# Earlier weight loads and splits for the first gate/up group, and later squares, in a two-layer encoder trunk

## The chip, the cores and the metric

The kernel runs on one core of a Trainium2 chip. The metric is device microseconds (us) of one execution, taken as the median of the runs; less is better.

## The reference

Each of two layers works on x, 256 positions by 2048 channels, in float32:

```
for l in range(DEPTH):
    h = rmsnorm(x, norm1_g[l])
    proj = jnp.einsum('bsd,de->bse', h, w_in[l])
    ...
    a = dilated_attention(q, k, v)
    g = chunked_spatial_gating(uv, gmlp_ln_g[l], w_spatial[l], b_spatial[l])
    mix = jnp.concatenate([rmsnorm(a, ...), rmsnorm(g, ...)], axis=-1)
    x = x + jnp.einsum('bse,ed->bsd', mix, w_out[l])
    h = rmsnorm(x, norm2_g[l])
    ff = jax.nn.silu(jnp.einsum('bsd,df->bsf', h, w_gate[l])) * jnp.einsum('bsd,df->bsf', h, w_up[l])
    x = x + jnp.einsum('bsf,fd->bsd', ff, w_down[l])
return rmsnorm(x, final_g)
```

The feed-forward width is 5632. What matters here is the passage in each layer from the second half of `w_out` (which adds the gMLP half `g` to x) to the first columns of `w_gate` and `w_up`, which need the normalised x.

## The kernel before, in words

**Products.** Every float32 operand is split into a high part (a copy rounded to the type that TensorE takes, made by ScalarE, line 861 for weights) and a low part (the difference, made by VectorE, line 862). A product is three matmuls: high by high, high by low, low by high. Positions lie in two tiles of 128, so four PSUM banks `v`, `z`, `x`, `w` hold two position tiles by two blocks of 512 columns.

**Groups and slots.** The work is a list of groups. In layer 0, groups 5 and 6 are `w_out` for the attention half, groups 7 and 8 (`og`) for the gMLP half, and groups 9, 10, 11 and so on (`ff`) are gate/up blocks of 512 columns each. A group is a list of slots, and slots are the unit of time of the schedule: each slot emits its matmuls, then a side task or two. An ordinary slot `N` is one pair of 128-row blocks for one position tile, so a pair takes two slots (24 matmuls together). In an `ff` group four of the eight pairs are done in a fast form: seven products M1 to M7 (12 matmuls each) of sums of weight blocks (`q11`, `q12`, `q21`, `q22`) with sums of x blocks. The first group of a layer takes the order N N N M1 N M5 M2 M6 M3 M7 M4; later ones take N M1 N M5 M2 N M6 M3 M7 M4 N.

**Loads and splits by slot number.** A weight load (1 MB each, issued by the SP queue) and a weight split have a due slot. Events are sorted by due slot less a lead, 5 slots for a load and 3 for a split (2 for a fast group after the first). At each slot the events that have come up are emitted, if the pool of 17 buffers of 1 MB has room. A load waits on its buffer's last readers. Each engine and queue works in the order of emission.

**What splits do besides.** After M1's split VectorE adds `q12` into `q11` (line 837). After M5's split VectorE adds `q22` into `q11`, and a DMA from GpSimd's queue adds `q22` into `q12` (line 841). After M2's split another such DMA adds `q11` into `q21`: M4's split can only start when it has landed. The sums `q11` of the second kind serve M6.

**The norm.** The x blocks (four of 512 channels) are finished by group 7 (blocks 0, 1) and group 8 (blocks 2, 3). For each block a side task `Norm.block` transposes on TensorE (line 265). Blocks 0 and 1 serve the ordinary pairs. Blocks 2 and 3 serve the fast pairs: ScalarE copies the transposes to a buffer `hr` (lines 328, 329), VectorE forms four sums (line 252), ScalarE splits off the high half of `h` (line 255) and VectorE the low half (line 257). M1 reads block 2 in its first six matmuls and block 3 in the last six. Afterwards `Norm.square` sums squares (line 310, ScalarE); after the last block VectorE and GpSimd make `rstd` (lines 314, 271, 272), which the first `silu` (line 623) needs.

**Banks.** Five PSUM buffers serve `v`, `z`, `x`, `w` and one of the products M1, M5, M6, M7 at a time. M1's and M5's results are copied out by ScalarE (line 917), so M5 can start after M1's copy and M6 after M5's copy. M7 starts after VectorE has added M2's bank (line 937).

The order of emission in one slot `s` is:

```
split_by(s)
while next_event(s, False):
    pass
gr.run(i)
...
run_side()
```

Of the kernel before, what the change touches and what calls it, by code (L numbers as in the profile page):

```python
# [27 lines left out]
KD = D // P  # L28
# [3 lines left out]
KR = 4  # L32
# [31 lines left out]
LA_LOAD = 5  # L64
LA_SPLIT = 3
# [38 lines left out]
def encoder_kernel(ctx: ExitStack, tc: tile.TileContext, x, xf, w, ws, lng, cols, fg, cs, msk, out):  # L104
# [18 lines left out]

    early = cpool.tile([P, 1], F32, name="early")
    nc.scalar.activation(out=early, in_=ones, func=AF.Copy)
    warm = sdp.tile([P, P], F32, tag="sd", name="warm")
    for _ in range(WARM):
# [29 lines left out]
    def gcol(l, which, k):  # L157
        return colt[:, l * GC + {"n1": 0, "a": KD, "g": KD + 8, "n2": KD + 16}[which] + k:][:, 0:1]
# [51 lines left out]
    def put_split(kt, k, src, g):  # L210

        hi = kt.t[:, k, 0, :]
        nc.scalar.activation(out=hi, in_=src, func=AF.Copy, scale=g)
        nc.vector.scalar_tensor_tensor(
            out=kt.t[:, k, 1, :], in0=src, scalar=g, in1=hi.bitcast(F32), op0=ALU.mult, op1=ALU.subtract
        )
        kt.ready[k] = True

    def put_splits(kt, k, ps, gs):

        src = [ps[:, j].rearrange("p t q -> p (t q)") for j in range(2)]
        for j in range(2):
            nc.scalar.activation(out=kt.t[:, k + j, 0, :], in_=src[j], func=AF.Copy, scale=gs[j])
        for j in range(2):
            nc.vector.scalar_tensor_tensor(
                out=kt.t[:, k + j, 1, :], in0=src[j], scalar=gs[j], in1=kt.t[:, k + j, 0, :].bitcast(F32),
                op0=ALU.mult, op1=ALU.subtract,
            )
            kt.ready[k + j] = True
# [14 lines left out]
    def sums(raw, n, dst):  # L244

        r = raw.view("p (j f q) -> p j f q", j=2, f=8)[:, :n]
        f = lambda i: r[:, :, i, :]
        for to, a, op, b in (
            (3, f(7), ALU.subtract, f(2)), (4, f(3), ALU.subtract, f(0)),
            (5, f(0), ALU.subtract, f(7)), (6, f(1), ALU.add, f(4)),  # L250
        ):
            nc.vector.tensor_tensor(out=f(to), in0=a, in1=b, op=op)
        src = r[:, :, 0:7, :].rearrange("p j f q -> p j (f q)")
        hi, lo = (dst.rearrange("p (j h z) -> p j h z", h=2, z=7 * P)[:, :, i] for i in range(2))
        nc.scalar.activation(out=hi, in_=src, func=AF.Copy)  # L255
        yield 1
        nc.vector.tensor_tensor(out=lo, in0=src, in1=hi.bitcast(F32), op=ALU.subtract)  # L257
        raw.free()

    def transposes(src, k, name):  # L260

        ps = sdp.tile([P, 2, NT, P], F32, tag="sd", name=name)
        for j in range(2):
            for t in range(NT):
                nc.tensor.transpose(ps[:, j, t, :], src[:, t, (k + j) * P:(k + j + 1) * P], ident)  # L265
        return ps
# [8 lines left out]
    class Norm:  # L275
# [41 lines left out]
        def block(self, b):  # L317

            fast = [p for p in (2 * b, 2 * b + 1) if p >= self.slow]
            raw = Big(f"hr_{self.which}_{self.l}_{b}") if fast else None  # L320
            ps = [transposes(xt[b], 2 * j, f"tpn_{self.which}_{self.l}_{2 * b + j}") for j in range(2)]
            yield 1
            for j in range(2):
                p = 2 * b + j
                g = [gcol(self.l, self.which, 2 * p + i) for i in range(2)]
                if p >= self.slow:
                    r = raw.view("p (j f q) -> p j f q", j=2, f=8)[:, j + len(fast) - 2]
                    nc.scalar.activation(out=r[:, 0:8:7, :], in_=ps[j][:, 0], func=AF.Copy, scale=g[0])
                    nc.scalar.activation(out=r[:, 1:3, :], in_=ps[j][:, 1], func=AF.Copy, scale=g[1])
                else:  # L330
                    put_splits(self.pairs[p], 0, ps[j], g)
                    self.ready[p] = True
            if fast:
                yield from sums(raw, len(fast), self.hs[:, (fast[0] - self.slow) * 14 * P:(fast[-1] + 1 - self.slow) * 14 * P])
                for p in fast:
                    self.ready[p] = True
            yield 1
            self.square(b)

        def early(self, k, src):  # L340

            put_split(self.pairs[k // 2], k % 2, src, gcol(self.l, self.which, k))
            self.ready[k // 2] = k % 2 == 1
# [601 lines left out]
    slots, loads, first_slot = [], [], {}  # L945
# [7 lines left out]
    splits, seen = [], set()  # L953
    for s, (gr, i) in enumerate(slots):
        for key in gr.chunks(gr.slots[i]):
            if (gr.g, key) not in seen:
                seen.add((gr.g, key))
                splits.append((s, gr, key))
    def early(gr):
        return 0  # L960


    events = sorted(
        [(s - LA_LOAD - early(gr), 0, i) for i, (s, gr, *_) in enumerate(loads) if i >= KD // KR]
        + [(s - (2 if gr.fast and gr.idx else LA_SPLIT) - early(gr), 1, i) for i, (s, gr, _) in enumerate(splits)]
    )
    pos = 0

# [41 lines left out]
    for b in range(KD // KR):  # L1010
        _, gr, key, width, o = loads[b]
# [106 lines left out]
```

## Time and profile before

| | |
|---|---|
| median of 3 runs | 2159.31 us (2158.47 to 2159.74) |
| the profiled execution | 2160.09 us |
| its span, first to last instruction | 2158.3 us |
| TensorE (PE) busy | 97% of the span |
| VectorE (DVE), ScalarE (ACT) busy | 71%, 50% |
| mean granted TensorE clock | 0.992 of full speed |

The span is what the views show; 1.79 us of the execution lie around it. A busy share is an average over stages, so what the change is worth is read from the two stretches, one in each layer, in which the first gate/up group runs: about 349 to 400 us in layer 0, and the same 1068 us later in layer 1. In a timeline row the bracket gives the engine's idle time ahead of the row, and what ended it. Numbers of a buffer are left out of its name there: `hi_M` and `lo_M` are the halves of M1 to M7, `hi` and `lo` those of an N pair, `hl` those of a group that is not fast.

### The profile page before, as it was taken

The page shows a single profiled execution, that of the slowest core. Times are in us where ns is not written, and L with a number is a line of the kernel's source. Part 1 is how long each engine was busy: PE and PEld are TensorE (multiplying, and loading weights), DVE is VectorE, ACT ScalarE, POOL GpSimd, SP SyncE. Part 2 cuts the span into 40 slices and gives each one's busy share as a digit, 9 for nine tenths or more (in the row PEclk, how much of TensorE's full clock was granted, in tenths as well). Part 3 has the DMA queues.
Part 4 walks back from the last instruction along what each step waited for, and adds up shares of the span by engine and source line. Part 5 has one row for each costly group of instructions (what it writes and reads, how often), then busy time and mean ns, then how long its engine had stood idle before and what let it go on. Part 6 is the DMA issues. An engine that isn't in the chain of part 4 may idle for free.

```text
span 2158.3 us, 23529 instructions
## 1 busy us (share of the span) xinstructions
PE 2100.5 (97%) x9432; PEld 1725.6 (80%) x9432; DVE 1525.8 (71%) x1388; ACT 1072.7 (50%) x1153; POOL 117.7 (5%) x108
## 2 busy tenths in 40 slices
PE   8999999999999999999999999999999999999997
PEld 7888887788888878888788788877888788788885
DVE  5577656886687588668655766668847875886684
ACT  6445545554455355445553555455534553554453
POOL 0220000000000000000002200000000000000000
PEclk9999999999999999999999999999999999999999
DMA  8444554676776667667544355556766665776772
GB/s 339 175 145 171 186 204 158 213 249 223 241 243 195 234 214 232 216 222 262 198 178 174 127 189 185 195 160 237 235 241 226 215 234 196 228 251 224 241 244 78
DMA packets 65134, 451.96 MB, mean 209 GB/s; under 512 B 7296, under 2 KB 7296, under 8 KB 11264
## 3 DMA queue, kind: packets, MB, share of 16 engines
q1 hardware_dynamic: 58688, 404.31, 50.1%
q0 software_dynamic: 6336, 46.14, 10.9%
q8 instruction: 74, 1.21, 0.2%
q14 instruction: 36, 0.29, 0.0%
HBM read 402.19 MB, written 2.10 MB: 187 GB/s over the span
## 4 chain that ended last, share of the span: by engine, by line
PE 50%; DVE 5%; issue 2%; ACT 2%; DMA 1%; DVEq 0%; POOLq 0%; POOL 0%; ACTq 0%
PE mm_v L884 12%; PE mm_z L884 11%; PE mm_x L884 11%; PE mm_w L884 10%; PE mm L884 5%; DVE lo_M L862 2%; DMA raw_q<-raw_q 1%; ACT hi_M L861 1%; DVE lo L862 1%; PE tpf L265 1%; DVE hl L862 0%; PE sp L449 0%; PE tpn_n L265 0%; DVE m L937 0%; PE op L489 0%
## 5 line engine op out<-in xcount | busy, mean ns | idle before, releaser
L862 DVE TENSOR_TENSOR hl<-raw,hl 128x1024 fp32r<-128x1024 f32 (+1 forms) x402 | 478.9, 1240 | 65.3 <-ACT hl L861 63.5
L861 ACT ACTIVATE hl<-raw 128x1024 fp32r<-128x1024 f32 (+1 forms) x402 | 399.6, 1048 | 129.2 <-PE mm_w L884 80.7
L862 DVE TENSOR_TENSOR lo_M<-raw_q,hi_M 128x2048 fp32r<-128x2048 f32 x154 | 348.8, 2287 | 77.3 <-ACT hi_M L861 72.5
L861 ACT ACTIVATE hi_M<-raw_q 128x2048 fp32r<-128x2048 f32 x154 | 287.3, 1910 | 108.2 <-DMA raw_q<-raw_q 82.6
L884 PE MATMUL mm<-hi_M,h_n 128*128 128x512 f32 x704 | 235.5, 395 | 8.2 <-ACT h_n L255 4.1
L862 DVE TENSOR_TENSOR lo<-raw,hi 128x2048 fp32r<-128x2048 f32 x88 | 201.1, 2285 | 41.9 <-ACT hi L861 31.5
L861 ACT ACTIVATE hi<-raw 128x2048 fp32r<-128x2048 f32 x88 | 167.1, 1907 | 54.4 <-PE mm_w L884 43.0
L884 PEld LDWEIGHTS mm<-hi_M,h_n 128*128 128x128 f32 x704 | 132.7, 189 | 38.0 <-DVE h_n L257 6.4
L884 PE MATMUL mm_v<-hl,ff 128*128 128x512 f32 x528 | 136.3, 392 | 2.7 <-ACT ff L234 2.7
L884 PE MATMUL mm<-lo_M,h_n 128*128 128x512 f32 x352 | 138.0, 392 | 0.0
L884 PE MATMUL mm_x<-hl,ff 128*128 128x512 f32 x528 | 134.9, 391 | 0.0
L884 PE MATMUL mm_z<-hl,ff 128*128 128x512 f32 x528 | 134.1, 389 | 0.0
L884 PE MATMUL mm_w<-hl,ff 128*128 128x512 f32 x528 | 134.1, 389 | 0.0
L884 PE MATMUL mm_v<-hi,hb_n 128*128 128x512 f32 x352 | 126.2, 399 | 0.0
L884 PE MATMUL mm_z<-hi,hb_n 128*128 128x512 f32 x352 | 124.3, 394 | 0.0
L884 PE MATMUL mm_x<-hi,hb_n 128*128 128x512 f32 x352 | 122.9, 390 | 0.0
L884 PE MATMUL mm_w<-hi,hb_n 128*128 128x512 f32 x352 | 122.7, 389 | 0.0
L884 PE MATMUL mm_v<-hl,h_n 128*128 128x512 f32 x420 | 113.7, 402 | 9.1 <-DVE hl L862 4.6
L884 PEld LDWEIGHTS mm_v<-hl,ff 128*128 128x128 f32 x528 | 98.0, 188 | 25.0 <-ACT ff L234 3.7
L884 PEld LDWEIGHTS mm_z<-hl,ff 128*128 128x128 f32 x528 | 99.1, 188 | 20.7
L884 PEld LDWEIGHTS mm_w<-hl,ff 128*128 128x128 f32 x528 | 99.1, 188 | 20.7
L884 PEld LDWEIGHTS mm_x<-hl,ff 128*128 128x128 f32 x528 | 98.5, 188 | 20.1
(207 smaller groups left out, 3368.4 us busy)
## 6 DMA issues: line engine op xcount, KB each, us to landing
raw<-in_w SPq DMA_DIRECT2D x287, 1024.0 KB, 4.9
raw_q<-in_w SPq DMA_DIRECT2D x88, 1024.0 KB, 6.8
raw_q<-raw_q POOLq DMA_DIRECT2D x44, 1024.0 KB, 7.8
xt<-in_x SPq DMA_DIRECT2D x4, 512.0 KB, 13.6
out<-xt SPq DMA_DIRECT2D x8, 256.0 KB, 3.1
xf<-in_xf SPq DMA_DIRECT2D x3, 512.0 KB, 9.6
raw<-in_w SPq DMA_DIRECT2D x4, 256.0 KB, 5.7
lw<-in_ws SPq DMA_DIRECT2D x2, 512.0 KB, 5.4
```

The lines of the kernel that those rows point to most:

```text
L265: nc.tensor.transpose(ps[:, j, t, :], src[:, t, (k + j) * P:(k + j + 1) * P], ident)
L861: nc.scalar.activation(out=hi[:, sl], in_=src[:, sl], func=AF.Copy)
L862: nc.vector.tensor_tensor(out=lo[:, sl], in0=src[:, sl], in1=hi[:, sl].bitcast(F32), op=ALU.subtract)
L884: nc.tensor.matmul(bank[0], lhsT=lhsT, rhs=rhs, start=bank[1], stop=stop)
```

## The change

Two edits. For the first `ff` group of each layer (index 0, groups 9 and 37) the lead of a load grows by six slots, and that of a split by four. And in `Norm.block` the squares of blocks 2 and 3 are taken five slots after the last split of the block, where it was one.

```
@@ -334,7 +334,7 @@
                 yield from sums(raw, len(fast), self.hs[:, (fast[0] - self.slow) * 14 * P:(fast[-1] + 1 - self.slow) * 14 * P])
                 for p in fast:
                     self.ready[p] = True
-            yield 1
+            yield 5 if fast else 1
             self.square(b)
@@ -956,13 +956,15 @@
-    def early(gr):
-        return 0
+
+    def ahead(gr, n):
+
+        return n if gr.what == "ff" and gr.idx == 0 else 0
     events = sorted(
-        [(s - LA_LOAD - early(gr), 0, i) for i, (s, gr, *_) in enumerate(loads) if i >= KD // KR]
-        + [(s - (2 if gr.fast and gr.idx else LA_SPLIT) - early(gr), 1, i) for i, (s, gr, _) in enumerate(splits)]
+        [(s - LA_LOAD - ahead(gr, 6), 0, i) for i, (s, gr, *_) in enumerate(loads) if i >= KD // KR]
+        + [(s - (2 if gr.fast and gr.idx else LA_SPLIT) - ahead(gr, 4), 1, i) for i, (s, gr, _) in enumerate(splits)]
     )
```

TensorE's order does not change. The other engines' does, in these places (a name such as `lo_9_M5_2791` is the low half of M5 of group 9; the last number only counts).

VectorE around the sums and splits of blocks 2 and 3 (`hr_n2_0_2`, `hr_n2_0_3`), before:

```order
L862 TENSOR_TENSOR lo_9_M1_2707<-raw_9_q11_2659,hi_9_M1_2706 128x2048
L837 TENSOR_TENSOR raw_9_q11_2659<-raw_9_q11_2659,raw_9_q12_2661 128x2048
L252 TENSOR_TENSOR hr_n2_0_2_2695<-hr_n2_0_2_2695 128x2x128 x4
L862 TENSOR_TENSOR lo_9_3_2746<-raw_9_3_2681,hi_9_3_2745 128x2048
L257 TENSOR_TENSOR h_n2_0_2330<-hr_n2_0_2_2695,h_n2_0_2330 128x2x896
L252 TENSOR_TENSOR hr_n2_0_3_2732<-hr_n2_0_3_2732 128x2x128 x4
L257 TENSOR_TENSOR h_n2_0_2330<-hr_n2_0_3_2732,h_n2_0_2330 128x2x896
L862 TENSOR_TENSOR lo_9_M5_2791<-raw_9_q11_2659,hi_9_M5_2790 128x2048
L837 TENSOR_TENSOR raw_9_q11_2659<-raw_9_q11_2659,raw_9_q22_2743 128x2048
```

The same place now:

```order
L757 SCALAR_TENSOR_TENSOR xt_3_100<-mm_8_w_2512,rstd_g_0_2290,xt_3_100 128x512
L862 TENSOR_TENSOR lo_9_M1_2660<-raw_9_q11_2567,hi_9_M1_2659 128x2048
L837 TENSOR_TENSOR raw_9_q11_2567<-raw_9_q11_2567,raw_9_q12_2569 128x2048
L862 TENSOR_TENSOR lo_9_3_2693<-raw_9_3_2597,hi_9_3_2692 128x2048
L862 TENSOR_TENSOR lo_9_M5_2697<-raw_9_q11_2567,hi_9_M5_2696 128x2048
L837 TENSOR_TENSOR raw_9_q11_2567<-raw_9_q11_2567,raw_9_q22_2627 128x2048
L252 TENSOR_TENSOR hr_n2_0_2_2714<-hr_n2_0_2_2714 128x2x128 x4
L257 TENSOR_TENSOR h_n2_0_2330<-hr_n2_0_2_2714,h_n2_0_2330 128x2x896
L252 TENSOR_TENSOR hr_n2_0_3_2746<-hr_n2_0_3_2746 128x2x128 x4
L257 TENSOR_TENSOR h_n2_0_2330<-hr_n2_0_3_2746,h_n2_0_2330 128x2x896
L862 TENSOR_TENSOR lo_9_M2_2793<-raw_9_q21_2657,hi_9_M2_2792 128x2048
```

The low half of the fourth N pair, M5's low half and its add have gone ahead of the sums, and M2's low half follows the norm at once.

ScalarE from the copy of M1's result to the first split of group 10, before:

```order
L917 ACTIVATE m1_9_2809<-mm_9_1_2796 128x512
L310 ACTIVATE sq_n2_0_3_0_2811,ssn_n2_0_2329<-xt_3_100 128x512
L310 ACTIVATE sq_n2_0_3_1_2813,ssn_n2_0_2329<-xt_3_100 128x512
L861 ACTIVATE hi_9_M2_2820<-raw_9_q21_2771 128x2048
L861 ACTIVATE hi_9_M6_2837<-raw_9_q11_2659 128x2048
L861 ACTIVATE hi_9_M3_2853<-raw_9_q22_2743 128x2048
L917 ACTIVATE m5_9_2870<-mm_9_5_2857 128x512
L861 ACTIVATE hi_9_M7_2874<-raw_9_q12_2661 128x2048
L623 ACT_TABLE_LOAD
L623 ACTIVATE sil_0_0_0_2893<-c11_9_2890,rstd_n2_0_2817 128x512
L861 ACTIVATE hi_9_M4_2895<-raw_9_q21_2771 128x2048
L861 ACTIVATE hi_10_0_2936<-raw_10_0_2872 128x2048
```

And now:

```order
L917 ACTIVATE m1_9_2814<-mm_9_1_2801 128x512
L861 ACTIVATE hi_9_M3_2816<-raw_9_q22_2627 128x2048
L861 ACTIVATE hi_9_M7_2820<-raw_9_q12_2569 128x2048
L861 ACTIVATE hi_9_M4_2848<-raw_9_q21_2657 128x2048
L917 ACTIVATE m5_9_2865<-mm_9_5_2852 128x512
L310 ACTIVATE sq_n2_0_2_0_2867,ssn_n2_0_2329<-xt_2_99 128x512
L310 ACTIVATE sq_n2_0_2_1_2869,ssn_n2_0_2329<-xt_2_99 128x512
L310 ACTIVATE sq_n2_0_3_0_2889,ssn_n2_0_2329<-xt_3_100 128x512
L310 ACTIVATE sq_n2_0_3_1_2891,ssn_n2_0_2329<-xt_3_100 128x512
L623 ACT_TABLE_LOAD
L623 ACTIVATE sil_0_0_0_2888<-c11_9_2885,rstd_n2_0_2895 128x512
L861 ACTIVATE hi_10_0_2936<-raw_10_0_2871 128x2048
```

M4's split, which waits for the second adding DMA, now stands ahead of M5's copy, and all four squares stand behind that copy, just ahead of the `silu` that needs their sum. On GpSimd's queue the power for `rstd` now stands behind the second adding DMA, where it stood between the two.

The SP queue's loads from the last pairs of group 8 to M1's `q11`, before:

```order
L831 DMA raw_8_1_2413<-in_w 128x2048
L831 DMA raw_8_2_2447<-in_w 128x2048
L831 DMA raw_8_3_2493<-in_w 128x2048
L831 DMA raw_9_0_2557<-in_w 128x2048
L831 DMA raw_9_1_2593<-in_w 128x2048
L831 DMA raw_9_2_2625<-in_w 128x2048
L831 DMA raw_9_q11_2659<-in_w 128x2048
```

And now:

```order
L831 DMA raw_8_1_2413<-in_w 128x2048
L831 DMA raw_9_0_2415<-in_w 128x2048
L831 DMA raw_8_2_2449<-in_w 128x2048
L831 DMA raw_9_1_2451<-in_w 128x2048
L831 DMA raw_8_3_2497<-in_w 128x2048
L831 DMA raw_9_2_2499<-in_w 128x2048
L831 DMA raw_9_q11_2567<-in_w 128x2048
```

Loads of group 9 have gone in between those of group 8. The first load of group 10 (`raw_10_0`) now takes M6's old buffer `q11`, so it waits for the second adding DMA, which reads it.

## Rows read from the trace of the kernel before

**Rows 1.** Who TensorE waited for: us in total, times, longest.

```profile
PE mm_v L884 <- DVE lo L862: 15.7, 16, 2.2
```

**Rows 2.** Timeline of TensorE, layer 0: start, us, what, idle before.

```profile
347.79 1.52 PE L884 MATMUL mm_w<-hl,g 128*128 128x512 f32 x6
...
367.27 0.39 PE L884 MATMUL mm<-hi_M,h_n 128*128 128x512 f32 x1
...
369.03 0.73 PE L884 MATMUL mm<-hi_M,h_n 128*128 128x512 f32 x2 [1.14 <-DVE h_n L257]
...
372.28 0.80 PE L884 MATMUL mm<-hi_M,h_n 128*128 128x512 f32 x1 [2.06 <-ACT h_n L255]
...
376.21 0.63 PE L884 MATMUL mm_v<-hi,hb_n 128*128 128x512 f32 x1
...
402.71 0.59 PE L884 MATMUL mm_v<-lo,hb_n 128*128 128x512 f32 x1 [2.17 <-DVE lo L862]
...
414.25 0.50 PE L884 MATMUL mm_v<-lo,hb_n 128*128 128x512 f32 x1 [1.43 <-DVE lo L862]
```

**Rows 3.** Timeline of TensorE, layer 1: the last of those places.

```profile
1482.53 0.50 PE L884 MATMUL mm_v<-lo,hb_n 128*128 128x512 f32 x1 [1.47 <-DVE lo L862]
```

**Rows 4.** Stretches: us, busy us (count) of PE, PEld, DVE, ACT, POOL; clock; DMA.

```profile
349.15:354.59 5.44, 5.44 (x25) 4.50 (x24) 5.44 (x5) 0.00 (x0) 0.00 (x0) 1.00 0.54 193
...
372.28:378.77 6.49, 5.65 (x12) 3.97 (x13) 5.31 (x3) 5.37 (x11) 0.00 (x0) 0.50 0.18 50
...
402.71:406.10 3.39, 3.39 (x9) 2.62 (x10) 3.06 (x5) 1.28 (x2) 0.00 (x0) 0.54 0.69 290
```

**Rows 5.** Timeline of VectorE, layer 0.

```profile
359.56 1.56 DVE L252 TENSOR_TENSOR hr_n<-hr_n 128x256 f32<-128x256 f32 x4 [1.93 <-ACT hr_n L329]
...
372.26 2.02 DVE L257 TENSOR_TENSOR h_n<-hr_n,h_n 128x1792 fp32r<-128x1792 f32 x1 [1.82 <-ACT h_n L255]
...
380.26 6.70 DVE L862 TENSOR_TENSOR lo_M<-raw_q,hi_M 128x2048 fp32r<-128x2048 f32 x3
...
400.38 2.28 DVE L862 TENSOR_TENSOR lo<-raw,hi 128x2048 fp32r<-128x2048 f32 x1
...
404.09 0.69 DVE L937 TENSOR_TENSOR m<-mm_x,m 128x512 f32<-128x512 f32 x1
```

**Rows 6.** Timeline of ScalarE, layer 0.

```profile
370.53 1.70 ACT L255 ACTIVATE h_n<-hr_n 128x1792 fp32r<-128x1792 f32 x1 [4.36 <-DVE hr_n L252]
...
376.95 0.62 ACT L310 ACTIVATE sq_n<-xt 128x512 f32<-128x512 f32 x1
...
378.32 5.51 ACT L861 ACTIVATE hi_M<-raw_q 128x2048 fp32r<-128x2048 f32 x3
...
391.33 1.28 ACT L623 ACT_TABLE_LOAD   x1 [3.00 <-DVE c L937]
392.63 0.72 ACT L623 ACTIVATE sil<-c,rstd_n 128x512 f32<-128x512 f32 x1
```

**Rows 7.** Timeline of GpSimd, layer 0: the power for `rstd`, the second adding DMA.

```profile
380.41 2.71 POOL L272 TENSOR_TENSOR rstd_n<-rstd_n,mhalf 128x2 f32<-128x2 f32 x1 [21.07 <-DVE rstd_n L271]
383.10 0.91 POOL L841 DMA_DIRECT2D raw_q<-raw_q  x1
```

**Rows 8.** DMAs issued in 382 to 386 us: KB each, us to landing.

```profile
raw_q<-raw_q POOLq DMA_DIRECT2D x1, 1024.0 KB, 7.2
```

**Rows 9.** DMAs issued in 853 to 855 us (a later `ff` group).

```profile
raw<-in_w SPq DMA_DIRECT2D x1, 1024.0 KB, 6.4
raw_q<-raw_q POOLq DMA_DIRECT2D x1, 1024.0 KB, 12.8
```

**Rows 10.** Line 841, all 44 adding DMAs: us from issue to landing.

```profile
DMA to landing us min/median/max: 6.9/7.8/12.9
```

**Rows 11.** Line 831, 300 to 312 us: group 8's last loads, ns of an issue.

```profile
L831 SPq DMA_DIRECT2D raw<-in_w x3: 328/328/328, 303.3 to 309.5; - x3
...
DMA to landing us min/median/max: 4.9/4.9/7.5
```

## The prediction

> **What bounds the kernel now.** The table of engines comes first: TensorE is busy for 97% of the span, so a change that adds no matmul and takes none away can only pay or cost through TensorE's waits. The view of whom TensorE waited for says where they are: the 16 waits of an ordinary pair's first bank for a low half from VectorE, 15.7 us in all, are the largest that touch this passage [rows 1]. TensorE's timeline shows the passage itself. The pitch first: 24 matmuls fill 5.44 us at the full clock [rows 4], 0.227 each, so a fast product of 12 takes 2.72. M1 begins at 367.27 and meets waits of 1.14 for the low half of block 2 and 2.06 for the high half of block 3, and the third ordinary pair (N3) follows at 376.21; nine slots on, after the group, there are two long waits in the second group, 2.17 at 402.71 and 1.43 at 414.25 [rows 2]. I call the last one **T**, the low half of the second group's second pair. Layer 1 has it at 1482.53, 1068.28 later [rows 3], so I work out layer 0 and take it twice. The reader is to see that T is a wait for VectorE: whatever TensorE loses or gains ahead of it is swallowed there, unless VectorE reaches T at another time. The gain is therefore the move of T, not the waits at M1. VectorE's timeline shows what sets it: the low half of group 10's first pair (`lo_10_0`) ends at 400.38 + 2.28 = 402.66, the add of the x bank stands at 404.09, and T starts 10.16 after that add's start, 11.59 after `lo_10_0` [rows 2, 5]. ScalarE's and GpSimd's timelines lead back from there: `lo_10_0` stands behind M4's low half, M4's split waits for the second adding DMA, and that was issued at 383.10, behind the power for `rstd` [rows 7], and landed 7.2 later [rows 8].
>
> **The change, part by part.** No matmul, no byte and no instruction is added or taken away; everything is a move.
>
> *Earlier loads.* Group 9's loads stand between group 8's. Group 8's last loads were issued until 309.5 and landed in at most 7.5 [rows 11]. Its last pair's matmuls end at 347.79 + 1.52 = 349.31 [rows 2], so they begin 5.44 earlier, at 343.9. Three 1 MB loads put ahead of the last one cost at most 3 x 7.5 if each is paid in full: 309.5 + 22.5 + 7.5 = 339.5. Cost nothing, hidden under group 8's products; without that cover it would be up to 7.5 per load. `raw_10_0`, which now waits for the second adding DMA, is issued at about 382 below and needed at 391: 9 us for a load of 4.9 to 7.5, hidden by 1.5 at least.
>
> *Earlier splits, VectorE.* VectorE now does M1's low half, its add, N3's weight low half, M5's low half and its add after `og`'s last x add, before it turns to the sums. `og`'s last product leaves TensorE at 349.31; the x add is about 0.7, as the bank add of that size [rows 5]; five full-width operations take 6.70/3 = 2.23 each [rows 5]. 349.31 + 0.7 + 11.2 = 361.2, with a small gap for the last product's end 361.4, where block 2's sums start (before: 359.56, 1.8 earlier). From then on the norm runs without a gap: sums 1.56 (362.95), ScalarE's high half 1.70 (364.7), low half 2.02 (366.75), sums of block 3 (368.3), high (370.05), low (372.1) [rows 5, 6]. Before, block 3's low half ended at 372.26 + 2.02 = 374.28, since two full-width operations stood between. M1 starts at 367.27 as before. Its first six matmuls need block 2 alone, so they run to 368.6; the seventh waits 1.4 for the high half, the ninth 1.6 for the low one, and M1 ends at 373.05 at the full clock. N3 gains 376.21 - 373.05 = 3.15.
>
> *The second adding DMA.* M2's low half now follows the norm at once: 372.1 + 2.2 = 374.3, and the DMA is issued at 374.4, 8.7 ahead of 383.10, since the power no longer stands before it on GpSimd. I take the 7.2 of its own row and a little more, 7.4: landed 381.8. M4's split takes 5.51/3 = 1.84 [rows 6], to 383.7, M5's copy, which now stands behind it, 0.5 to 0.6 (a ScalarE pass of 512 columns, as the square [rows 6]), to 384.2. M6 needs the bank that M5's copy frees. TensorE would reach M6 at 373.05 + 5.44 + 2 x 2.72 = 383.95, so it waits about 0.3. M6, M3, M7, M4 take 10.9 from 384.3: M4 ends at 395.2.
>
> *Later squares.* The squares of two blocks now stand behind M5's copy. Two of them took 378.32 - 376.95 = 1.37 [rows 6], four 2.75: 386.95. Two small VectorE steps 0.4 (my estimate, from a wider add at 0.69 [rows 5]; nothing to 0.8), 387.3; the power 2.71 [rows 7], 390.0. The table load of 1.28, which now waits for nothing, lies under the power; `silu` 0.72 [rows 6] ends at 390.8, M3's bank is done before (384.3 + 5.44 = 389.75, add 0.7). The split of `raw_10_0` ends at 392.6, `lo_10_0` at 394.9. Before it was 402.66: 7.75 earlier, though `silu` itself comes only 2.5 us earlier. What stands behind it on VectorE, two adds, ends at 396.35, against M4's end at 395.2: the x add is late by neither. T comes at 394.9 + 11.6 = 406.5, 7.75 ahead of 414.25. TensorE still waits in the second group (about 1.1 at its M1, 1.8 at T), because it is early too, but those waits are inside the 7.75.
>
> *The clock.* Over 372.28 to 378.77, after the waits of 1.14 and 2.06, the granted clock was 0.50 (the lower level, 1.2 GHz), and over 402.71 to 406.10, after the wait of 2.17, it was 0.54 [rows 4]. The new waits at M1, 1.4 and 1.6 close together, are of that kind, so I expect the lower level again from about 372, but with no wait after it, for as long as the shorter row: 3.39 us at half pace, 1.7 lost. M6's wait of 0.3 takes up some, M4 ends at 396.6, after the two adds' 396.35: T moves by 0.2 to 406.7. The gain is 7.55 in a layer; behind T nothing differs.
>
> **Sum.** 2160.09 - 2 x 7.55 = 2145.0 for an execution like the profiled one; the median lies 0.8 below it, so 2144.2.
>
> **A rule against it.** The second adding DMA is issued while VectorE runs without a pause, in both kernels; before, VectorE was busy from 380.26 to 386.96 [rows 5] and the DMA issued at 383.10 landed in 7.2 all the same, ahead of 390.3 [rows 7, 8]. The Trainium skill, "SBUF — State Buffer", section "Who interferes with whom", says that VectorE can hold a port that it shares with GpSimd, so that a DMA from GpSimd's queue is starved while its descriptors are written; it excepts the two-input operation used here only by inference. The row sides with the exception. Were the DMA held until VectorE pauses, it would now wait for M6's, M3's and M7's low halves, 374.3 + 6.7 = 381.0, land at 388.4, and leave 7.75 - 6.6 = 1.15 a layer: 2157.0. By the row it would have landed after 394 before, so I give this 0.03.
>
> **Rivals.**
> - *The clock costs more* (0.23). The lower level lasts as long after M1 as the longer row, 6.49: 3.4 lost, 0.3 taken up, M4 ends at 398.3 and T moves by 1.9, to 408.4. Or it falls at the wait of about 1.8 before T and 1.7 is lost where nothing takes it up. One or the other in both layers 2147.2 to 2148, both 2151.
> - *The adding DMA is slow* (0.06). Of 44 the median took 7.8 and one 12.9 [rows 10]; the row with 12.8 had a 1 MB load issued with it [rows 9]. Here the next load waits for this very DMA, which speaks against it. At 12.9, landed 387.3, 2.25 is left a layer: 2154.8.
> - *Nothing is won* (0.05). The new chain DMA, M4's split, M5's copy, squares, power, `silu`, `hi_10_0` is one line with no slack; if the squares, the power or the table load together take 6 to 8 more than their rows, T stays: about 2159.
> - *Slower* (0.04). M5's copy stands behind M4's split, in order, so a late DMA stops M6 and with it TensorE, which it could not before. It decides from a landing 7.4 + 7.75 = 15.15 us after the issue; at 20 us it costs 4.85 a layer: 2169. No row is above 12.9 [rows 10].
>
> **How the numbers follow.** The forecast, 2142 to 2146.5 by itself (its bounds: DMA 6.9 to 7.8, the two small steps 0 to 0.8, the clock's 1.7 or none), has 0.59. Range 2141 to 2151.5: it holds the first two cases, 0.82, and ends where both costs of the clock come together. About 0.2%, 4.3 us, is what a measurement can tell from no change. Faster (below 2155.0): 0.59 + 0.23 + half of the slow DMA, 0.85; same: the other half, the rule and nothing won, 0.11; slower 0.04.
>
> **What the profile after would show.** Right: block 2's sums at about 361.4 behind M5's add; block 3's low half ending near 372.1; N3 near 373; the second adding DMA issued near 374.4, landed near 382; M6's wait under 0.5; no wait of 2.17 for `lo_10_0`; T near 406.6, and in layer 1 near 1482.53 - 2 x 7.6 = 1467. Wrong: a DMA landing behind VectorE's run; a wait of more than 1 us at M6 for M5's copy; `silu` later than 391; granted clock at 0.5 after 376 or after T; group 8's matmuls waiting for loads.

## The result, and the profile after

The changed kernel takes 2142.77 us (median of 4 runs, 2141.25 to 2144.14), the kernel before 2159.52 in the runs taken with it: a ratio of 0.9924, with a 95% interval of 0.9912 to 0.9936. The forecast was 2144.2, the range 2141 to 2151.5. The profiled execution took 2142.80, its span is 2141.0, against 2158.3.

Part 1 of the page of the changed kernel: the same instructions, and TensorE 9.5 us less busy than before (2100.5). Most of that is time at the lower clock that is gone: the mean granted clock is 0.996, where it was 0.992, and 0.004 of the span is 8.6 us (an estimate from these numbers).

```profile
PE 2091.0 (98%) x9432; PEld 1720.0 (80%) x9432; DVE 1526.3 (71%) x1388; ACT 1073.3 (50%) x1153; POOL 113.7 (5%) x108
```

TensorE's timeline of the changed kernel at the places of [rows 2, 3], with the first product of `og` (304.42), the transposes of x block 1 (333.40), M6 (386.54) and M1 of layer 1 (1427.77) besides:

```profile
304.42 1.52 PE L884 MATMUL mm_v<-hl,g 128*128 128x512 f32 x6
...
333.40 0.63 PE L265 MATMUL tpn_n<-ident,xt 128*128 128x128 f32 x4 [0.26 <-DVE hb_n L225]
...
348.87 1.52 PE L884 MATMUL mm_w<-hl,g 128*128 128x512 f32 x6
...
368.35 0.39 PE L884 MATMUL mm<-hi_M,h_n 128*128 128x512 f32 x1
...
371.08 0.50 PE L884 MATMUL mm<-hi_M,h_n 128*128 128x512 f32 x1 [1.20 <-ACT h_n L255]
...
373.14 1.22 PE L884 MATMUL mm<-hi_M,h_n 128*128 128x512 f32 x2 [1.33 <-DVE h_n L257]
...
375.01 0.63 PE L884 MATMUL mm_v<-hi,hb_n 128*128 128x512 f32 x1
...
386.54 0.39 PE L884 MATMUL mm<-hi_M,h_n 128*128 128x512 f32 x1
...
407.78 0.50 PE L884 MATMUL mm_v<-lo,hb_n 128*128 128x512 f32 x1 [1.51 <-DVE lo L862]
...
1427.77 0.39 PE L884 MATMUL mm<-hi_M,h_n 128*128 128x512 f32 x1
...
1466.06 0.50 PE L884 MATMUL mm_v<-lo,hb_n 128*128 128x512 f32 x1 [1.52 <-DVE lo L862]
```

The kernel before at the two of these places that were not shown, the first product of `og` and M1 of layer 1:

```profile
303.82 1.52 PE L884 MATMUL mm_v<-hl,g 128*128 128x512 f32 x6
...
1435.46 0.39 PE L884 MATMUL mm<-hi_M,h_n 128*128 128x512 f32 x1
```

From M1's start to T, layer 0 took 414.25 - 367.27 = 46.98 us before [rows 2] and takes 407.78 - 368.35 = 39.43 now: 7.55 less. Layer 1 took 1482.53 - 1435.46 = 47.07 and takes 38.29: 8.78 less. Within M1 there were three waits before (1.14, 2.06 and a third of 0.84 that [rows 2] leave out) and there are two now. The wait of 2.17 ahead of T is gone; the wait at T itself has stayed.

VectorE in the changed kernel, layer 0: block 2's sums, block 3's low half, the z bank's add, `lo_10_0`, the x bank's add.

```profile
362.35 1.55 DVE L252 TENSOR_TENSOR hr_n<-hr_n 128x256 f32<-128x256 f32 x4
...
371.06 2.03 DVE L257 TENSOR_TENSOR h_n<-hr_n,h_n 128x1792 fp32r<-128x1792 f32 x1 [1.82 <-ACT h_n L255]
...
392.18 0.69 DVE L937 TENSOR_TENSOR m<-mm_z,m 128x512 f32<-128x512 f32 x1 [1.30 <-PE mm_z L884]
...
393.64 2.28 DVE L862 TENSOR_TENSOR lo<-raw,hi 128x2048 fp32r<-128x2048 f32 x1
...
397.62 0.69 DVE L937 TENSOR_TENSOR m<-mm_x,m 128x512 f32<-128x512 f32 x1 [0.36 <-PE mm_x L884]
```

ScalarE there: M4's split, M5's copy, the `silu`, the split of group 10's first pair.

```profile
382.91 1.92 ACT L861 ACTIVATE hi_M<-raw_q 128x2048 fp32r<-128x2048 f32 x1 [3.45 <-DMA raw_q<-raw_q]
384.73 0.58 ACT L917 ACTIVATE m<-mm 128x512 f32<-128x512 f32 x1
...
389.50 0.72 ACT L623 ACTIVATE sil<-c,rstd_n 128x512 f32<-128x512 f32 x1
390.12 1.90 ACT L861 ACTIVATE hi<-raw 128x2048 fp32r<-128x2048 f32 x1
```

GpSimd there, the second adding DMA and the power for `rstd`, in the other order than in [rows 7]:

```profile
375.84 0.88 POOL L841 DMA_DIRECT2D raw_q<-raw_q  x1 [18.40 <-DVE lo_M L862]
388.67 0.71 POOL L272 TENSOR_TENSOR rstd_n<-rstd_n,mhalf 128x2 f32<-128x2 f32 x1 [11.95 <-DVE rstd_n L271]
```

The DMA issues of the changed kernel in 373 to 380 us (KB each, us to landing), for [rows 8]:

```profile
raw_q<-raw_q POOLq DMA_DIRECT2D x1, 1024.0 KB, 7.0
```

The reader is to see in these rows who is waited for now. Between M1's end and M4's end in layer 0 TensorE waits for nobody; M6 follows M2 without a gap, 1.2 us after M5's copy has ended. VectorE, just ahead of and just behind `lo_10_0`, waits for TensorE, for the z bank (1.30) and for the x bank (0.36), and T comes 407.78 - 397.62 = 10.16 after the x add, exactly as in [rows 2, 5]. So M4's end sets the x add, the x add sets T, and what still delays M4 in layer 0 are the two waits at M1 and the clock behind them.

Layer 1 differs in one place. M5's copy and M6 there:

```profile
1444.04 0.58 ACT L917 ACTIVATE m<-mm 128x512 f32<-128x512 f32 x1
```

```profile
1444.67 0.50 PE L884 MATMUL mm<-hi_M,h_n 128*128 128x512 f32 x1
```

The copy ends at 1444.62 and M6 starts 0.05 later. TensorE was not slowed here, reached M6 before the copy was done and lost 0.2 on it; M6 starts 16.90 after M1's start (18.19 in layer 0). At the full clock the line from the second adding DMA to M5's copy comes that much too late for TensorE.

Stretches of the changed kernel (columns as in [rows 4]): two at M1's waits and behind them in layer 0, then a part of layer 1's attention, where the change moves nothing, then M1's waits in layer 1.

```profile
371.90:375.30 3.40, 2.16 (x5) 1.79 (x6) 3.40 (x3) 2.78 (x3) 0.00 (x0) 0.65 0.00 0
375.30:378.70 3.40, 3.40 (x14) 2.71 (x14) 3.20 (x2) 3.40 (x3) 0.88 (x1) 0.85 0.57 116
...
1224.50:1233.50 9.00, 8.18 (x42) 6.84 (x43) 7.58 (x11) 5.70 (x9) 0.00 (x0) 1.00 0.35 131
...
1431.10:1434.50 3.40, 2.08 (x9) 1.62 (x9) 3.40 (x2) 3.40 (x4) 0.00 (x0) 1.00 0.00 0
```

And the stretch of the kernel before that answers to the one in layer 1's attention:

```profile
1231.00:1240.00 9.00, 8.13 (x35) 6.69 (x36) 7.58 (x11) 5.81 (x9) 0.00 (x0) 0.81 0.19 60
```

The whole difference of the spans, 17.3, is then: M1 of layer 0 begins 1.08 later (+1.08), M1 to T in layer 0 -7.55, from T to T of layer 1 (1482.53 - 414.25) - (1466.06 - 407.78) = -10.00, behind it (2158.3 - 1482.53) - (2141.0 - 1466.06) = -0.83. Of the -10.00, -8.78 lie between M1 and T and -1.22 ahead of M1. Ahead of M1 some 1.7 of gain are the clock, not the change: over 9 us of layer 1's attention the granted clock was 0.81 in the one execution and 1.00 in the other, 9 x 0.19 = 1.7, after the same two waits (0.97 and 1.26; 0.98 and 1.26). The -0.83 behind the second T lies at two waits for low halves in later groups, one of 0.34 that is gone and one of 0.90 that is now 0.55; nothing was moved there.

### The profile page after: what moved, and what is told of

It is laid out like the page before. It is cut to its first block, busy times and chain, and to the rows that moved or that the text cites. A ratio compares the mean times of both kernels' runs of the same rounds, so it can differ in the third digit from the quotient of the medians.

```text
span 2141.0 us, 23535 instructions
## 1 busy us (share of the span) xinstructions
PE 2091.0 (98%) x9432; PEld 1720.0 (80%) x9432; DVE 1526.3 (71%) x1388; ACT 1073.3 (50%) x1153; POOL 113.7 (5%) x108
## 4 chain that ended last, share of the span: by engine, by line
PE 83%; DVE 8%; issue 4%; ACT 3%; DMA 2%; SPq 0%; DVEq 0%; POOLq 0%; POOL 0%; ACTq 0%
PE mm_v L884 19%; PE mm_z L884 19%; PE mm_x L884 19%; PE mm_w L884 16%; PE mm L884 8%; DVE lo_M L862 3%; DVE lo L862 1%; ACT hi_M L861 1%; DVE hl L862 1%; PE tpf L265 1%; DMA raw_q<-raw_q 1%; DMA raw<-in_w 1%; PE sp L449 1%; DVE rb_k L419 0%; PE op L489 0%
```

## Experiments

All times are medians with the ratio to the kernel before on the same chip. Edits are shown against the changed kernel, and `...` stands for code that is left out. The changed kernel itself was not run again on these chips; the kernel before took 2158.33 beside `e1`, `e2`, `e3` and `e7`, 2159.89 beside `e4`, `e5`, `e8` and `e9`, and 2161.26 beside `e10`, against 2159.52 beside the changed kernel, so a difference to 2142.77 can be off by about 1 us.

**The earlier loads and splits alone** (`e1`):

```
-            yield 5 if fast else 1
+            yield 1
```

> The earlier loads and splits alone; squares one slot after the split, as before. Theory A (the trace after: TensorE runs from M1's end to M4's end without a wait, and M4's end sets the x add and T; the squares have slack where they stand now): two squares (1.5 us) stand ahead of M2's split again, so the second adding DMA is issued about 1.2 us later than in the changed kernel, M5's copy comes about 1.2 us later, just when TensorE wants its bank, M6 waits at most 0.3: the same as the changed kernel within 0.5 us, about 2143.2. Theory B (as the prediction had it: DMA, M4's split, copy, squares, silu, lo_10_0 are one line): the four squares leave that line, lo_10_0 comes earlier, but the x add stays bound by M4: also about 2143, M6's wait near 1. A rival C (the squares carry the gain): near 2159.

Measured: 2143.02, ratio 0.9932 [0.9919, 0.9944]. M5's copy on ScalarE and M6 on TensorE in this kernel:

```profile
385.66 0.57 ACT L917 ACTIVATE m<-mm 128x512 f32<-128x512 f32 x1
```

```profile
368.03 0.39 PE L884 MATMUL mm<-hi_M,h_n 128*128 128x512 f32 x1
...
386.29 0.50 PE L884 MATMUL mm<-hi_M,h_n 128*128 128x512 f32 x1
```

The copy ends at 386.23, M6 starts 0.06 later: it comes just when TensorE wants it, the cost that A gave. The time is that of the changed kernel within the noise: the second edit has no share in the gain that could be measured. C is out; A and B gave nearly the same time here, so this run does not tell them apart.

The profiled execution had the lower clock behind M1's waits in both layers (39.63 and 39.51 from M1 to T). The copy ends 18.20 after M1's start, and at the full clock M6 started 16.90 after it. So where the clock stays up, the squares at their old place should cost about 1.3 us a layer; that is an estimate from these rows, and no run shows it.

**The later squares alone** (`e2`): both `ahead` numbers 0.

```
-        [(s - LA_LOAD - ahead(gr, 6), 0, i) ...
+        [(s - LA_LOAD - ahead(gr, 0), 0, i) ...
-        ... - ahead(gr, 4), 1, i) ...
+        ... - ahead(gr, 0), 1, i) ...
```

> The later squares alone; loads and splits as before. M2's split is 1.4 us earlier, the adding DMA is issued about 381 instead of 383.1 (no power ahead of it); but the squares now stand ahead of the silu and of M4's split on ScalarE, with the reduction, the power and the silu between: M4's split starts 0.5 us earlier to 2 us later than before. A and B: 2157 to 2162, no gain. C (the squares carry the gain): 2145 to 2150.

Measured: 2159.33, ratio 1.0007 [0.9998, 1.0016]: no gain, as A and B said. M1's start in this kernel, from which its rows are to be counted (before: 367.27), and GpSimd:

```profile
365.10 0.39 PE L884 MATMUL mm<-hi_M,h_n 128*128 128x512 f32 x1
```

```profile
379.56 0.88 POOL L841 DMA_DIRECT2D raw_q<-raw_q  x1 [22.38 <-DVE lo_M L862]
390.61 0.71 POOL L272 TENSOR_TENSOR rstd_n<-rstd_n,mhalf 128x2 f32<-128x2 f32 x1 [10.17 <-DVE rstd_n L271]
```

and M4's low half on VectorE:

```profile
393.91 2.29 DVE L862 TENSOR_TENSOR lo_M<-raw_q,hi_M 128x2048 fp32r<-128x2048 f32 x1 [3.39 <-ACT hi_M L861]
```

Counted from M1's start, the DMA is issued 14.46 after it, before 15.83, so 1.4 earlier. But M4's split stands behind the squares, the power and the `silu` on ScalarE, and its low half starts 28.8 after M1's start, before 27.9 (at 395.19): it does not come earlier for it.

**The earlier loads alone** (`e3`): the splits' number 0, `yield 1`.

```
-            yield 5 if fast else 1
+            yield 1
-        ... - ahead(gr, 4), 1, i) ...
+        ... - ahead(gr, 0), 1, i) ...
```

> The earlier loads alone; splits and squares as before. The orders on VectorE and ScalarE in the passage are nearly those of before, so A and B expect 2159 within 1.5 us. If loads were what M1 waited for, 2150 or less.

Measured: 2158.42, ratio 0.9996 [0.9987, 1.0005]. The earlier loads alone change nothing; they are there so that the splits can be early. With `e1`, 15 us belong to the earlier splits, given the earlier loads. (The splits without the loads were not tried: they would come up before their loads.) GpSimd's power for `rstd` took 2.71 in this kernel, as long as before.

**The squares twice** (`e7`):

```
                 nc.scalar.activation(out=junk, ..., func=AF.Square, accum_out=self.ss[:, t, b:b + 1])
+                if b * 2 >= self.slow and self.slow < KD // 2:
+                    nc.scalar.activation(out=junk, ..., func=AF.Square, accum_out=self.ss[:, t, b:b + 1])
```

> The changed kernel with each square of blocks 2 and 3 of the second norm taken twice (3.0 us more of ScalarE work between M5's copy and the silu, in each layer). Theory A: the silu has 2.6 us of slack before the z bank is ready, lo_10_0 1.6, the x add 0.4, so T comes about 1.0 us later in each layer: about 2145. Theory B (one line with no slack, as in the prediction): the 3.0 us arrive at T whole, 6 us in both layers: 2148.8.

Measured: 2146.02, ratio 0.9945 [0.9932, 0.9957]; 3.0 above `e1` on the same chip and 3.25 above the changed kernel, for 6.0 us of work put into the line. VectorE in this kernel, `lo_10_0` and the x bank's add:

```profile
394.31 2.29 DVE L864 TENSOR_TENSOR lo<-raw,hi 128x2048 fp32r<-128x2048 f32 x1 [0.51 <-ACT hi L863]
...
398.03 0.69 DVE L939 TENSOR_TENSOR m<-mm_x,m 128x512 f32<-128x512 f32 x1
```

Now `lo_10_0` waits for ScalarE's split and the x add no longer for TensorE; the two adds behind `lo_10_0` end at the x add's start. So the line has become the bound, but only after some 1.5 us of slack a layer, 3.0 of work less half of the 3.0 to 3.25 that arrived. The time lies between A's 2145 and B's 2148.8, nearer to A.

**The add behind the sums** (`e4`): the first group's `q11 += q22` moved into the gap of VectorE behind block 2's sums.

```
             elif key == "M5":
-                self.add("q11", "q22")
+                if self.what == "ff" and self.idx == 0:
+                    state["add"] = lambda: self.add("q11", "q22")
+                else:
+                    self.add("q11", "q22")
...
         nc.scalar.activation(out=hi, in_=src, func=AF.Copy)
+        state.pop("add", lambda: None)()
         yield 1
```

> The changed kernel with the first group's add of q22 into q11 moved behind block 2's sums on VectorE, into the gap of 1.8 us in which VectorE waits for ScalarE's high half. Theory A (M1's waits go through M4's end to T, since TensorE waits nowhere between): the norm's chain ends 1.3 us earlier, M1's waits fall from 2.5 to about 1.2, T comes 1.3 earlier in each layer, up to 2.4 if the clock no longer falls: 2138 to 2140.5. Theory B (T is set by VectorE's or ScalarE's own chain, M1's waits are swallowed): 2142.5 to 2143.5.

Measured: 2137.79, ratio 0.9899 [0.9886, 0.9913]. VectorE and TensorE in this kernel, and the stretch around M1's wait:

```profile
360.18 1.56 DVE L252 TENSOR_TENSOR hr_n<-hr_n 128x256 f32<-128x256 f32 x4 [0.53 <-ACT hr_n L330]
361.65 2.29 DVE L838 TENSOR_TENSOR raw_q<-raw_q,raw_q 128x2048 f32<-128x2048 f32 x1
```

```profile
367.90 0.39 PE L888 MATMUL mm<-hi_M,h_n 128*128 128x512 f32 x1
...
371.25 0.74 PE L888 MATMUL mm<-hi_M,h_n 128*128 128x512 f32 x2 [1.33 <-DVE h_n L258]
...
404.84 0.50 PE L888 MATMUL mm_v<-lo,hb_n 128*128 128x512 f32 x1 [1.51 <-DVE lo L863]
```

```profile
369.70:373.10 3.40, 2.07 (x9) 1.53 (x9) 3.40 (x2) 3.40 (x3) 0.00 (x0) 1.00 0.00 0
```

M1 has one wait of 1.33 in place of two, the clock stays at 1.00 behind it, and the time is 5.0 less, just past the end of the range that A gave for an undisturbed clock. B's time is out. From M1's start to T layer 0 takes 404.84 - 367.90 = 36.94 and layer 1 36.84. The changed kernel took 38.29 where its clock stayed up and 39.43 where it did not: some 1.4 a layer are the moved add, and up to 1.1 more the clock that no longer falls.

The edit brings M2's low half and the second adding DMA forward as well, from 7.5 to 6.05 after M1's start, so this run alone does not tell by which branch T comes earlier. That it is M4's end is read from the waits for the z and x banks above and from `e7`; and M4 needs both, for in layer 1 M6 already started with the end of M5's copy.

**The first split at its old lead** (`e5`):

```
+    def late(gr, k):
+        return 0 if k == 0 else ahead(gr, 4)
...
-        ... - ahead(gr, 4), 1, i) for i, (s, gr, _) in enumerate(splits)]
+        ... - late(gr, k), 1, i) for i, (s, gr, k) in enumerate(splits)]
```

> The changed kernel with the split of the first weight block of each first group back at its old lead, so that VectorE's low half of it no longer stands ahead of the low halves of x blocks 0 and 1, for which TensorE's transposes waited 0.26 us. Theory A: the 0.48 us that each layer lost ahead of M1 come back, 1.0 in all: about 2141.8. Rival: they are swallowed at M1, whose waits grow by as much (VectorE sets its end): 2142.8.

Measured: 2141.86, ratio 0.9919 [0.9905, 0.9932]. Its interval overlaps that of the changed kernel, so the time alone does not tell the two apart; TensorE's timeline does.

```profile
301.73 1.52 PE L884 MATMUL mm_v<-hl,g 128*128 128x512 f32 x6
...
329.85 1.03 PE L265 MATMUL tpn_n<-ident,xt 128*128 128x128 f32 x8
...
365.18 0.39 PE L884 MATMUL mm<-hi_M,h_n 128*128 128x512 f32 x1
```

The transposes run without a wait, and from `og`'s first product to M1 it is 63.45 us, as before (367.27 - 303.82), where the changed kernel takes 63.93. M1's waits do not grow for it (1.19 and 1.32), so the 0.48 is real in the trace. This execution kept the full clock behind M1's waits in both layers, and took 38.37 and 38.35 from M1 to T; layer 1's stretch:

```profile
1426.70:1430.10 3.40, 2.12 (x9) 1.78 (x10) 3.40 (x3) 3.40 (x4) 0.00 (x0) 1.00 0.00 0
```

**The second group's add behind the next pair** (`e8`): `q11 += q12` after the next split's low half, in all `ff` groups but the first of a layer.

```
-            if key == "M1":
+            if key == "M1" and self.idx:
+                state["behind"] = lambda: self.add("q11", "q12")
+            elif key == "M1":
                 self.add("q11", "q12")
...
             self.hl[key] = (own, hi, lo)
+            state.pop("behind", lambda: None)()
```

> The changed kernel with the add of q12 into q11 moved behind the next pair's low half on VectorE in every gate/up group but the first of a layer. Theory A: T's low half comes 2.2 us earlier, its wait of 1.5 us goes in both layers, and the next product waits up to 0.5: 2140.5 to 2141.5, less if the waits of 0.55 and 0.96 in later groups shrink too. Rival: M5's split, which now waits 2.2 us longer for the add, gives it all back or more: 2143 to 2150.

Measured: 2138.15, ratio 0.9900 [0.9886, 0.9913]. Whom TensorE waited for in this kernel (total, times, longest), the first line:

```profile
PE mm_v L887 <- DVE lo_M L862: 10.4, 20, 1.1
```

The 14 waits of 11.1 us for an ordinary pair's low half, T among them, are gone, and waits for a fast product's low half have grown from 5.8 to 10.4. The sum is 6.5 us less; the time is 4.6 less, 2.4 more than the better end of A's range, which counted the waits at the two T and left the other groups open.

**The last three together** (`e9`):

> The three changes of the other kernels of this set together. Theory A: their gains add, since each takes another wait: 2143 less 2.6 to 4.8, less 1.0, less 1.5 to 2.5: about 2136. If the wait at T is what the earlier M1 runs into, 2139 to 2141.

Measured: 2132.65, ratio 0.9874 [0.9861, 0.9888], the fastest kernel of the study. The single gains, 5.0 + 0.9 + 4.6 = 10.5, come to 10.1 together, so they add, as A said: they are three different waits. A's 2136 was too high since `e4` and `e8` had each given more than was expected of them.

**Subtracts beside the power** (`e10`): four subtracts on VectorE, whose result is used nowhere, one run.

```
                 self.rstd = rstd_of(tot, D, f"{self.which}_{self.l}")
+                if self.which == "n2":
+                    for i in range(4):
+                        junk = s2p.tile([P, NB], F32, ...)
+                        nc.vector.tensor_tensor(out=junk, in0=xt[0][:, 0, :], in1=xt[1][:, 0, :], op=ALU.subtract)
```

> The changed kernel with four subtracts of 128x512 from SBUF put on VectorE behind the scale that the power for rstd waits for, in each layer, so that VectorE works with two SBUF inputs while GpSimd takes the power (their result is used nowhere). In the kernel before, the power took 2.71 us beside a VectorE subtract of 2.3 us, in the changed kernel 0.71 beside an idle VectorE. Theory P (GpSimd waits for the VectorE instruction that runs, then goes): the power takes about 0.7 to 1.5. Theory Q (it is held for VectorE's whole unbroken run, 2.7 us): about 3.4. Rival N (the 2.71 had another cause): 0.71. The end of the group moves by less than 1.5 us a layer, since VectorE has 2.2 us of idle time there.

Measured: 2146.1 in one run, which is for the rows and not for the time. GpSimd's power and the subtracts on VectorE:

```profile
387.95 1.08 POOL L272 TENSOR_TENSOR rstd_n<-rstd_n,mhalf 128x2 f32<-128x2 f32 x1 [11.95 <-DVE rstd_n L271]
```

```profile
387.77 2.87 DVE L319 TENSOR_TENSOR dummy<-xt,xt 128x512 f32<-128x512 f32 x4
```

The power has grown from 0.71 to 1.08, in both layers; in layer 0 it ends 0.54 after the first subtract (387.77 + 2.87/4 = 388.49, power's end 389.03) and well ahead of the run's end at 390.64. P holds; Q and N are out.

## Why the prediction was right, step by step

Everything in layer 0 stands 1.08 later than in the kernel before from `og`'s last product on (348.87 against 347.79), so 1.08 is taken off the times of after here, unless they are said to be the trace's own.

- *The norm's chain*: right. Block 2's sums at 361.27 (361.4 forecast), block 3's low half ended at 372.01 (372.1), M1's waits 1.20 and 1.33 (1.4 and 1.6). The forecast counted from start to start at 0.227 a matmul, and so counted they are 371.08 - 368.35 - 6 x 0.227 = 1.37 and 373.14 - 371.08 - 2 x 0.227 = 1.61; the bracket counts from the modelled end of the matmul ahead.
- *The second adding DMA*: right. Issued 374.76 (374.4), landed for M4's split at 381.83 (381.8), 7.0 us after the issue, and so it was not held. In layer 0 that says little: in the trace's own time the DMA was issued at 375.84 and VectorE's run had a pause at 377.49. Layer 1 has the clean case:

```profile
1432.41 8.95 DVE L862 TENSOR_TENSOR lo_M<-raw_q,hi_M 128x2048 fp32r<-128x2048 f32 x4
```

```profile
1435.24 0.86 POOL L841 DMA_DIRECT2D raw_q<-raw_q  x1 [18.59 <-DVE lo_M L862]
```

```profile
raw_q<-raw_q POOLq DMA_DIRECT2D x1, 1024.0 KB, 6.9
```

VectorE ran without a pause until 1441.36, 6.1 us past the issue, and the DMA landed 6.9 us after it all the same. By the rule of the Trainium skill, "SBUF — State Buffer", section "Who interferes with whom", without its exception for this kind of operation, whose reason it marks as inferred, the DMA would have been held until then; the rows side with the exception.
- *The clock*: right in kind in layer 0, 0.65 and 0.85 in the two stretches at and after the waits, so the lower of the two levels (1.2 GHz) for a part of each, and N3 at 373.93 where 373.05 was forecast for the full clock. In layer 1, after the same waits of 1.20 and 1.32, it stayed at 1.00, and from M1 to T layer 1 took 1.14 less than layer 0. So the lower level came once in this execution and not twice, which the forecast did not have. Its net price was forecast at 1.4, 1.7 less the 0.3 that M6 would have waited anyway. M6's wait was right for the full clock: in layer 1 M6 followed M2 by 0.2 more than the pitch, with the end of the copy.
- *T*: 7.55 earlier from M1 on, as forecast (406.70 after the shift, 406.7), but not all by the way that was forecast. The term of the power was mis-sized: 2.71 was taken from a row in which the power waited for VectorE, and it took 0.71. The `silu` so ended at 389.1 and not 390.8, and was not the last to be waited for: `lo_10_0` stood behind the z bank's add, for which VectorE waited 1.30 on TensorE. M3 came later by the clock and the `silu` sooner by the power, and by luck the two gave the forecast's 394.9 within 0.1. Layer 1, where the clock did not fall, shows the miss: T came 8.78 earlier and not the 7.75 that `lo_10_0` allowed for at the full clock. That all the steps from the DMA to `lo_10_0` are "one line with no slack" was wrong; `e7` put 3.0 us a layer into it, of which about half arrived. T was where it was forecast in layer 0 since the other branch, M4's end to the x add, was worked out as well (396.6; measured 396.54).
- *The earlier splits* were put at nothing on the way to M1, and that was wrong by 0.48 a layer: the low half of group 9's first weight block now stands on VectorE ahead of the low halves of x blocks 0 and 1, and TensorE's transposes wait 0.26 for them. `e5` takes it away.
- *The squares edit* was costed as part of the line; it has no measurable share (`e1`, `e2`), though at the full clock it may have a small one (the estimate at `e1`). That both edits together remove the power from ahead of the DMA is true, but `e1` removes it as well, since the splits alone bring the DMA ahead of it.
- *The sum* was 1.4 too high against the median. In the profiled execution 15.1 were forecast and 17.3 came: 7.55 and 8.78 between M1 and T, less 0.48 twice for the transposes, less 0.6 that this execution began `og` later for (304.42 against 303.82, of which 0.3 is a longer wait for the first weights), plus 1.7 of clock in layer 1's attention and 0.8 in two waits behind the second T. So 15.4 of the 17.3 belong to the passage and 1.9 to chance between the two executions: that the sum comes so near to the 15.1 is in part luck, since the 0.48 twice that it left out and layer 1's 1.2 more than forecast nearly cancel.

What `e4`, `e5`, `e8` and `e9` show of the bound: TensorE's waits at M1, at the transposes and at T are time that is left in this passage, and each became shorter or went by moving one VectorE operation behind another that TensorE waits for.

## What to carry to other kernels

When several engines work in program order, ask of each operation on the busy one not only whether it is early enough but what stands behind it: here one add of 2.3 us moved into another wait was worth 5 us over the two layers, 2.8 of it at the same clock, and one split moved too far forward cost 0.5 a layer. Work out every branch that ends at the place where the time is decided, since the one that looks longest may have slack, and take a duration only from a row in which the engine was not itself waiting inside the instruction. To see whether an edit has a share, run the edits apart: here one of the two did all that could be measured.

## What the runs showed of the hardware

The power of 256 elements on GpSimd took 0.71 us beside an idle VectorE (changed kernel, `e2`), 2.71 when a VectorE subtract of 2.3 us from SBUF had begun 0.15 before it [rows 5, 7], and 1.08 beside subtracts of 0.7 (`e10`): it ends about 0.54 to 0.63 after the end of the VectorE instruction that ran, and is not held for the following ones. The profile books this wait as busy time of GpSimd. The Trainium skill, "SBUF — State Buffer", section "Who interferes with whom", says that a VectorE instruction with two SBUF inputs contends with a GpSimd instruction that reads SBUF; the rows agree with it, and the price in them is the rest of the one instruction. In the changed kernel the adding DMA from GpSimd's queue was not delayed beside such instructions (6.9 us under a run of VectorE that went on for 6.1 us of it).

The clock after like waits differed inside one execution: 0.65 after 1.20 and 1.33 in layer 0, 1.00 after 1.20 and 1.32 in layer 1. It differed between executions too: after waits of the same size it fell in both layers in `e1` (39.63 and 39.51 us from M1 to T) and in neither in `e5` (38.37 and 38.35). It makes about 1.1 us in a layer here, so by estimate up to some 2 us between executions of one kernel; what decides it these runs do not show.
